# A decoder block on one core: the pairs of the channel mixer reordered, gelu's product moved to a rotating PSUM bank

## The chip, the cores and the metric

The kernel runs on one core of a Trainium2 chip. The metric is the device time of one execution in microseconds: the median of three runs before is 828.67 us (828.44 to 828.79). Engines are named as the profile names them: PE (TensorE, matmuls) with PEld (its weight loads), DVE (VectorE), ACT (ScalarE), POOL (GpSimd), SP (which issues the transfers).

## The reference

One layer of a hybrid decoder trunk on 512 tokens of 1024 channels. Two mixers and their merge come first, then the part that the change touches, the channel mixer, and a per-layer embedding:

```python
hf = rmsnorm(x, norm_ffn[i])
up = causal_dwconv(hf @ w_up[i], ffn_dw_w[i], ffn_dw_b[i])
gate, val = jnp.split(up, 2, axis=-1)
x = x + (jax.nn.gelu(gate) * val) @ w_down[i]
```

`w_up` is 1024 x 5632 (2816 columns of gate and 2816 of value), `w_down` 2816 x 1024, and the convolution has three taps along the tokens.

## The kernel before

Every product is made of three matmuls of fp32r parts: an operand is cut into a high part (ACT, `hi_of`, L118) and a low part, the operand minus its high part (`lo_of`, L121, on DVE, in one place on POOL), and high x high, high x low and low x high are summed in PSUM.

The channel mixer works in 22 pairs (`Pair`). Pair f makes 128 columns of gate and the 128 columns of value that belong to them, for all 512 tokens. With the inputs split in two halves (blocks of four 128-row tiles), the tokens in two halves of 256 (LO and HI) and gate against value, this is a 2 x 2 by 2 x 2 block product, and it is done with seven block products instead of eight (m1 to m7; each is 4 x 3 = 12 matmuls of 128x128 by 128x256). The price is sums of weight blocks: blocks 11 and 21 are the halves of the gate's columns, 12 and 22 those of the value's; POOL forms t1 and t2 ("a") and t3 and t4 ("b"), four subtractions of 128x512 per pair (L306). So a pair has four weight tiles to cut: "11" (128x1024, blocks 11 and 21), "t12" and "t34" (128x1024, the sums), and "22" (128x512, block 22).

The list `pieces` gives the order in which weights are fetched, summed, cut and used. `Stream` walks it: `pump` issues what has room (at most four cut tiles are held, three buffers `tt` hold sums), `work` emits the next stage of a cut (a high part, or the low part that follows it), `take` and `done` bracket the use of a tile by PE.

A slot is one block product with what is emitted beside it: `slot` calls the product, `st.work()`, the copy given as `then`, `st.pump()` and `step()`, which moves each tail one yield on. In a middle pair the slots are m6, m2, m1 of the next pair, m7, m5 of the next pair, m3, m4. Each pair accumulates in a PSUM bank for gate and one for value; two of each alternate. Of the eight banks the other four rotate (`ps()`). The seeds carry m1 of the next pair into its banks: `seed_value` (L1329) goes to value HI, before m6; `seed_gate` (L1332) to gate LO, before m2. After m6 its result is copied to value LO (L1344), after m7 value HI is copied to gate HI (L1353).

The tail of a pair (`after`) runs beside the next pair: m5 is added to value (DVE L1375), ACT makes the first taps of value (`uv`, L1380) and gate (`ug`, L1382), DVE the other two taps of each (L1367), ACT gelu (L1387), DVE the product (L1389, into `uv` in SBUF), and the product is cut into the operand `a` of the down product. `seed_value` has to wait until uv's taps have read the value bank, `seed_gate` until the product has read the gate bank.

The down product comes in three groups, at pair 8, at pair 15 and at the end (`rows_product`): two sweeps of 512 columns, each over all its weights and four token tiles of 128, and after a sweep `done` adds each tile's bank to the residual (DVE L1259). The next sweep, and the m1 after it, take the same four rotating banks.

Of the kernel before, what the change touches and what calls it, by code (L numbers as in the profile page):

```python
# [83 lines left out]
def block_kernel(ctx: ExitStack, tc: tile.TileContext, x, p, rel_bias, norm_mix, w_in, conv_dw_w, conv_dw_b,  # L84
# [103 lines left out]
    def up_sums(*names):  # L188
        for name, f in names:
            pieces.append(((name, f), None, 4 if name == "22" else KC, P, "add" if name in ("a", "b") else "sum"))  # L190
# [9 lines left out]
    for f in range(1, NF):  # L200
        if f + 1 < NF:
            up_raw(f + 1)
            up_sums(("a", f + 1), ("b", f + 1), ("11", f + 1))
        if f in DOWN_IN:
            f0, f1 = DOWN_IN[f]
            rows_pieces("down%d" % f0, w_down, list(range(f0, f1)))
        up_sums(("t34", f))
        if f + 1 < NF:
            up_sums(("t12", f + 1))
        up_sums(("22", f))  # L210
    rows_pieces("down%d" % FFN_GROUPS[-1][0], w_down, list(range(*FFN_GROUPS[-1])))
    ple_piece(1)
    rows_pieces("gate", w_ple_gate, list(range(KC)))
# [3 lines left out]
    class Stream:  # L217
# [8 lines left out]
        def pump(self, force=False, most=9):  # L226

            most += self.cuts
            while self.stages:
                self.work()  # L230
            while self.cuts < min(self.dmas, most) and (force or self.asked[self.cuts] < self.call):
                i = self.cuts
                key, _, a, b, tag = pieces[i]
                if tag in ("first", "second"):
                    self.blocks(key[1], self.raw[i], tag)
                elif tag == "add":
                    if self.stages or not self.adds:
                        break
                    self.adds -= 1
                    self.add(*key)  # L240
                elif tag == "sum":
                    src, at = self.sums[key]
                    if self.hls >= self.limit or self.call < at:
                        break
                    hl = work("whl", (P, 2, a, b), F32R, tag="whl", bufs=CUT)
                    self.hl[i] = hl
                    self.cut(hl, src, a, nc.gpsimd if key[0] == "22" and key[1] not in DOWN_IN else nc.vector)
                    self.hls += 1
                    self.seconds -= key[0] == "22"
                    self.raws -= key[0] == "11"  # L250
                elif tag is not None:
                    if tag == "whl" and self.hls >= self.limit:
                        break
                    hl = work("whl", (P, 2, a, b), F32R, tag=tag, bufs=CUT if tag == "whl" else 1)
                    self.hl[i] = hl
                    self.cut(hl, self.raw[i], a)
                    self.hls += tag == "whl"
                    self.raws -= key != ("ple", 0)
                self.cuts += 1
            while self.dmas < len(pieces):  # L260
                i = self.dmas
                key, srcs, a, b, tag = pieces[i]
                if tag in ("sum", "add"):
                    self.asked[i] = self.call
                    self.dmas += 1
                    continue
                if key == ("ple", 0):

                    ple[0] = work("ple", (P, NT, 512))
                    raw = ple[0][:, 2:4, :]  # L270
                else:
                    n, home, most = self.raws, "wraw", 2
                    if tag is None:
                        n, home = self.wholes, "pT"
                    elif tag == "second":
                        n, home = self.seconds, "second"
                        if key[1] > 2:
                            home, most = "pT" if key[1] % 2 else "second", 3
                    if n == most:
                        break  # L280
                    raw = work("wraw", (P, a, b), tag=home, bufs=2)
                    self.raws += tag not in (None, "second")
                c = 0
                for src in srcs:
                    n = src.shape[-1]
                    nc.sync.dma_start(raw[:, :, c:c + n], src)
                    c += n
                self.raw[i], self.asked[i] = raw, self.call
                self.seconds += tag == "second"
                self.wholes += tag is None  # L290
                self.dmas += 1
            self.call += 1
# [894 lines left out]
    def rows_product(name, ks, a_of, done, late=None, filler=None, between=None, last=None, banks=None, order=range(NT),  # L1187
# [3 lines left out]
        for n in range(2):  # L1191
# [8 lines left out]
            for i in range(0, len(ks), 2):  # L1200
                kk = ks[i:i + 2]
                st.pump()
                hl = st.take(name, n, ks[i])
                hls.append((kk, hl))
                if n == 0 or late is None:
                    for t in range(NT):
                        part(t, kk, hl)
                        st.work()
                    st.done()
            if n == 0 or late is None:  # L1210
                if late and name != "gate" and not cut_on:
                    st.pump()
                for t in range(NT):
                    done(t, n, o[t])
                    if late and name != "gate" and not cut_on and t == 1:
                        st.work()
                continue
            if between:
# [88 lines left out]
    def fw(k, c):  # L1307
        return ffnw[k // 2][:, (k % 2) * 44 + c:(k % 2) * 44 + c + 1]
# [7 lines left out]
    class Pair:  # L1316


        def __init__(self, f):
            self.f, self.gate, self.value = f, gates[f % 2], values[f % 2]  # L1320
            self.b1 = None

        def m1(self):
            self.first = ps()
# [6 lines left out]
        def seed_gate(self):  # L1331
            nc.scalar.activation(self.gate[:, LO], self.first[:, LO], AF.Copy)  # L1332

        def m5(self):
            self.t12 = st.take("t12", self.f)
            o = ps()
            mm_block(o[:, LO], self.t12, 0, hf["s1"], True)
            self.m5_ = work("m5", (P, 256), tag="sc", bufs=2)
            nc.scalar.activation(self.m5_, o[:, LO], AF.Copy)

        def m6(self):
            mm_block(self.value[:, HI], self.t12, 4, hf["s2"], False)
            st.done()
            nc.scalar.activation(self.value[:, LO], self.value[:, HI], AF.Copy)  # L1344

        def m2(self):
# [22 lines left out]
        def after(self):  # L1369

            f, c = self.f, NF + self.f
            uv, ug = [work(name, (P, 512), tag="S", bufs=8) for name in ("uv", "ug")]
            v = self.value
            halves = lambda a: a.rearrange("p (h t) -> p h t", h=2)
            nc.vector.tensor_tensor(halves(v), halves(v), self.m5_.unsqueeze(1).broadcast_to((P, 2, 256)),  # L1375
                                    op=ALU.add)
            yield
            yield
            yield
            nc.scalar.activation(uv, v, AF.Identity, scale=fw(2, c), bias=fw(3, c))  # L1380
            yield
            nc.scalar.activation(ug, self.gate, AF.Identity, scale=fw(2, f), bias=fw(3, f))  # L1382
            self.taps(uv, v, c)
            yield
            self.taps(ug, self.gate, f)
            yield
            nc.scalar.activation(self.gate, ug, AF.Gelu_apprx_tanh)  # L1387
            yield
            nc.vector.tensor_tensor(uv, self.gate, uv, op=ALU.mult)  # L1389
            yield  # L1390
            a = act[f] = work("a", (P, 2, 512), F32R, tag="act", bufs=8)
            hi_of(a[:, 0], uv)
            yield
            yield
            lo_of(a[:, 1], uv, a[:, 0])

    gain_f = load_gain(norm_ffn)
    for t in range(NT):
# [53 lines left out]
    def slot(product, then=None, cut=True):  # L1452

        product()
        st.work()
        if then:
            then()
        if cut:
            st.pump()
        step()  # L1460
# [10 lines left out]
    for f in range(NF):  # L1471
# [11 lines left out]
        else:  # L1483
            cut = f not in DOWN_IN
            slot(this.m6, cut=cut)
            if f > 1:
                slot(this.m2, cut=cut)
            else:
                step()
            if f + 1 < NF:  # L1490
                coming = pairs[f + 1] = Pair(f + 1)
            if f in DOWN_IN:
                coming.b1 = st.take("11", f + 1)
                step()
                st.pump(most=1)
                step()
                st.work()
                drain()
                down(*DOWN_IN[f], None)
            if f + 1 < NF:  # L1500
                slot(coming.m1)
            slot(this.m7)
            if f + 1 < NF:
                slot(coming.m5, coming.seed_value)
        tails.append(this.after())
        slot(this.m3)
        slot(this.m4, coming.seed_gate if 0 < f < NF - 1 else None)
    drain()
    gain_p = load_gain(norm_ple)
# [89 lines left out]
```

## Time and profile before

| | |
|---|---|
| median of three runs | 828.67 us (828.44 to 828.79) |
| the profiled execution | 829.38 us |
| its span, first to last instruction | 827.6 us |
| granted TensorE clock, mean | 0.997 |
| PE busy | 802.1 us, 97% |
| DVE busy | 606.1 us, 73% |
| ACT busy | 442.8 us, 54% |
| POOL busy | 190.4 us, 23% |
| stage of the pairs and the two downs inside it | 400 to 722 us |

A timeline row reads: start, duration, engine, source line, operation, tile written and tiles read, shapes, and in brackets the idle time of the engine just before with what ended it. A duration includes the time in which an instruction that has started is held back. The distance of two starts on one engine is a little shorter than the duration, since the next instruction begins while the last one still writes. Matmul ends are modelled, so PE is read from start to start.

### The profile page before, as it was taken

Reading aid. Unit: us, or ns where it says so; the run is one execution under the profiler, and the core shown is the slowest. Engines: PE = TensorE matmul, PEld = TensorE weight load, DVE = VectorE, ACT = ScalarE, POOL = GpSimd, SP = SyncE. Lnnn points to the kernel's source line nnn. Section 1 sums busy time; section 2 is a strip of 40 time slices with the busy share of each in tenths; the row PEclk is TensorE's granted clock in tenths of the full one; section 3 lists DMA queues with packets and bytes.
Section 4 is the critical chain, followed back from the end, with each engine's and each line's share of the span. In section 5 each row is a group of like instructions: output and inputs, shape, how many; then the busy total and the mean of one; then the engine's idle time right before and its main releaser. Section 6 shows DMA issues by size and latency. Waiting matters only on the chain.

```text
span 827.6 us, 12258 instructions
## 1 busy us (share of the span) xinstructions
PE 802.1 (97%) x4688; PEld 695.1 (84%) x4688; DVE 606.1 (73%) x965; ACT 442.8 (54%) x839; POOL 190.4 (23%) x183
## 2 busy tenths in 40 slices
PE   7999999999999999999989999999999999999996
PEld 5888888888888876887789998799987899888885
DVE  5469987988987897935779986359984389855664
ACT  6331624287778874432666774147762277634443
POOL 2000000000010000005477661046640266201012
PEclk9999999999999999999999999999999999999998
DMA  7246777411110113452043323413324232231322
GB/s 219 78 119 186 184 191 177 94 52 52 51 51 27 51 52 107 146 205 76 27 129 102 103 77 116 140 51 102 103 77 134 70 104 77 77 127 52 129 75 103
DMA packets 108070, 84.69 MB, mean 102 GB/s; under 512 B 4113, under 2 KB 93641, under 8 KB 108011
## 3 DMA queue, kind: packets, MB, share of 16 engines
q1 hardware_dynamic: 108010, 83.90, 34.7%
q8 instruction: 37, 0.61, 0.3%
q14 instruction: 23, 0.18, 0.1%
HBM read 79.36 MB, written 2.43 MB: 99 GB/s over the span
## 4 chain that ended last, share of the span: by engine, by line
PE 68%; DVE 16%; ACT 9%; issue 3%; POOL 2%; DMA 1%; SPq 0%; POOLq 0%; ACTq 0%; DVEq 0%
PE ps L128 9%; PE ps L130 9%; PE ps L129 9%; PE ps L142 8%; PE ps L143 8%; PE ps L141 8%; ACT whl L118 5%; DVE whl L121 5%; DVE a L121 3%; DVE ug L1367 3%; DVE uv L1367 3%; PE ps L868 2%; PE ps L894 2%; PE ps L135 2%; PE ps L137 2%
## 5 line engine op out<-in xcount | busy, mean ns | idle before, releaser
L121 DVE TENSOR_TENSOR whl<-wraw,whl 128x512 fp32r<-128x512 f32 (+1 forms) x140 | 133.7, 968 | 84.0 <-ACT whl L118 80.5
L135 PE MATMUL ps<-hf,whl 128*128 128x256 f32 x616 | 176.3, 286 | 4.7 <-ACT ps L1332 2.4
L118 ACT ACTIVATE whl<-wraw 128x512 fp32r<-128x512 f32 (+1 forms) x160 | 123.6, 794 | 101.5 <-PE ps L143 36.0
L137 PE MATMUL ps<-hf,whl 128*128 128x256 f32 x616 | 174.7, 284 | 2.3 <-DVE whl L121 1.8
L136 PE MATMUL ps<-hf,whl 128*128 128x256 f32 x616 | 174.2, 283 | 0.0
L135 PEld LDWEIGHTS ps<-hf,whl 128*128 128x128 f32 x616 | 118.0, 192 | 8.5 <-ACT ps L1332 4.8
L137 PEld LDWEIGHTS ps<-hf,whl 128*128 128x128 f32 x616 | 118.1, 192 | 3.2 <-DVE whl L121 2.5
L136 PEld LDWEIGHTS ps<-hf,whl 128*128 128x128 f32 x616 | 118.1, 192 | 0.0
L128 PE MATMUL ps<-hT,whl 128*128 128x512 f32 x256 | 101.9, 398 | 0.0
L130 PE MATMUL ps<-hT,whl 128*128 128x512 f32 x256 | 100.2, 391 | 0.3 <-DVE whl L121 0.3
L129 PE MATMUL ps<-hT,whl 128*128 128x512 f32 x256 | 99.9, 390 | 0.0
L734 DVE SCALAR_TENSOR_TENSOR acc<-aT,convw,acc 128x512 f32<-128x512 f32 x120 | 86.2, 747 | 1.0
L306 POOL TENSOR_TENSOR tt<-wraw 128x512 f32<-128x512 f32 x44 | 65.7, 1494 | 77.1 <-DVE whl L121 71.9
L121 DVE TENSOR_TENSOR whl<-tt,whl 128x1024 fp32r<-128x1024 f32 x44 | 58.5, 1334 | 24.4 <-ACT whl L118 23.8
L142 PE MATMUL ps<-whl,a 128*128 128x512 f32 x176 | 69.6, 396 | 1.2 <-DVE whl L121 1.2
L141 PE MATMUL ps<-whl,a 128*128 128x512 f32 x176 | 69.7, 396 | 0.7 <-DVE x L1259 0.7
L143 PE MATMUL ps<-whl,a 128*128 128x512 f32 x176 | 69.4, 395 | 0.0
L306 POOL TENSOR_TENSOR tt<-wraw,tt 128x512 f32<-128x512 f32 x44 | 60.0, 1364 | 9.3 <-DVE whl L121 6.0
L118 ACT ACTIVATE whl<-tt 128x1024 fp32r<-128x1024 f32 x44 | 46.0, 1045 | 22.0 <-PE ps L143 19.0
L130 PEld LDWEIGHTS ps<-hT,whl 128*128 128x128 f32 x256 | 48.0, 188 | 11.2 <-DVE whl L121 0.7
L128 PEld LDWEIGHTS ps<-hT,whl 128*128 128x128 f32 x256 | 48.1, 188 | 9.0 <-issue 0.2
L129 PEld LDWEIGHTS ps<-hT,whl 128*128 128x128 f32 x256 | 48.2, 188 | 8.7
(214 smaller groups left out, 1529.1 us busy)
## 6 DMA issues: line engine op xcount, KB each, us to landing
wraw<-in_w_up SPq DMA_DIRECT2D x44, 512.0 KB
wraw<-in_w_in SPq DMA_DIRECT2D x32, 512.0 KB
wraw<-in_w_down SPq DMA_DIRECT2D x20, 512.0 KB
wraw<-in_w_out SPq DMA_DIRECT2D x8, 512.0 KB
wraw<-in_w_ple_gate SPq DMA_DIRECT2D x8, 512.0 KB
W<-vdram SPq DMA_DIRECT2D x8, 264.0 KB
xin<-in_x SPq DMA_DIRECT2D x4, 512.0 KB
wraw<-in_w_ck SPq DMA_DIRECT2D x4, 512.0 KB
```

The source lines that it names most:

```text
L118: nc.scalar.activation(dst, src, AF.Copy, scale=scale)
L121: engine.tensor_tensor(dst, src, f32(hi), op=ALU.subtract)
L128: nc.tensor.matmul(o, hl[:, 0, j, cs], a_hi, start=start, stop=False)
L129: nc.tensor.matmul(o, hl[:, 0, j, cs], a_lo, start=False, stop=False)
L130: nc.tensor.matmul(o, hl[:, 1, j, cs], a_hi, start=False, stop=stop)
L135: nc.tensor.matmul(o, hl[:, 0, j0 + k, :], a[:, 0, k, :], start=start and k == 0, stop=False, skip_group_check=True)
L136: nc.tensor.matmul(o, hl[:, 0, j0 + k, :], a[:, 1, k, :], start=False, stop=False, skip_group_check=True)
L137: nc.tensor.matmul(o, hl[:, 1, j0 + k, :], a[:, 0, k, :], start=False, stop=k == 3, skip_group_check=True)
L141: nc.tensor.matmul(o, a_hi, w_hi, start=start, stop=False)
L142: nc.tensor.matmul(o, a_hi, w_lo, start=False, stop=False)
L143: nc.tensor.matmul(o, a_lo, w_hi, start=False, stop=stop)
L306: sub = lambda to, x_, y_: nc.gpsimd.tensor_tensor(to, x_, y_, op=ALU.subtract)
```

## The change

- In the tail, gate comes before value: first taps on ACT, then the taps on DVE; gelu follows ug's taps directly, with uv's taps beside it.
- Gelu's product goes to a rotating PSUM bank instead of `uv`, and the high and low part of `a` are cut from there (not in the last pair before a down and in the last two pairs, which write `uv` as before). High and low part of `a` come one and two yields earlier.
- The low part of block 22 is DVE's in every pair; POOL only makes sums.
- In `slot` the copy (`then`) is emitted before `st.work()`; `seed_value` comes after m3 instead of after m5.
- In `rows_product` a sweep without `late` (the two downs inside) adds the residual of a token tile right after that tile's last product.
- At the end, m1 of the last pair takes the slot of m5 in the pair before it, m5 of the last pair runs in its own pair between m7 and m3, and the pieces "11" and "t12" of the last pair are listed later. `take_t12` lets m5 and m6 come in either order.

What DVE runs in a middle pair, from the product that closes one tail to the taps of the next (before). `whl` is a cut weight tile, `tt` a sum, `wraw` a raw weight, `a` the cut product:

```order
L1389 TENSOR_TENSOR uv_4222<-ps_3343,uv_4222 128x512
L1375 TENSOR_TENSOR ps_3346<-ps_3346,m5_4201 128x512
L121 TENSOR_TENSOR whl_4345<-wraw_4091,whl_4345 128x1024
L121 TENSOR_TENSOR whl_4367<-tt_4167,whl_4367 128x1024
L121 TENSOR_TENSOR whl_4385<-tt_4292,whl_4385 128x1024
L121 TENSOR_TENSOR a_4369<-uv_4222,a_4369 128x512
L1367 SCALAR_TENSOR_TENSOR uv_4350<-ps_3346,ffnw0_819,uv_4350 128x511
L1367 SCALAR_TENSOR_TENSOR uv_4350<-ps_3346,ffnw0_819,uv_4350 128x510
L1367 SCALAR_TENSOR_TENSOR ug_4351<-ps_3344,ffnw0_819,ug_4351 128x511
L1367 SCALAR_TENSOR_TENSOR ug_4351<-ps_3344,ffnw0_819,ug_4351 128x510
```

And after:

```order
L1386 SCALAR_TENSOR_TENSOR uv_4226<-ps_3345,ffnw0_819,uv_4226 128x510
L1410 TENSOR_TENSOR ps_4351<-ps_3343,uv_4226 128x512
L1394 TENSOR_TENSOR ps_3346<-ps_3346,m5_4200 128x512
L121 TENSOR_TENSOR whl_4347<-wraw_4091,whl_4347 128x1024
L121 TENSOR_TENSOR a_4353<-ps_4351,a_4353 128x512
L121 TENSOR_TENSOR whl_4372<-tt_4168,whl_4372 128x1024
L121 TENSOR_TENSOR whl_4389<-tt_4294,whl_4389 128x1024
L121 TENSOR_TENSOR whl_4404<-wraw_4019,whl_4404 128x512
L1386 SCALAR_TENSOR_TENSOR ug_4356<-ps_3344,ffnw0_819,ug_4356 128x511
L1386 SCALAR_TENSOR_TENSOR ug_4356<-ps_3344,ffnw0_819,ug_4356 128x510
L1386 SCALAR_TENSOR_TENSOR uv_4355<-ps_3346,ffnw0_819,uv_4355 128x511
L1386 SCALAR_TENSOR_TENSOR uv_4355<-ps_3346,ffnw0_819,uv_4355 128x510
```

ug's taps stand before uv's, the low part of `a` reads `ps` and stands behind the low part of "11", and a 128x512 low part from `wraw` (block 22) has joined the three others, behind the low part of t12.

ACT in the same stretch before, from the copy of m5 to the high part of block 22:

```order
L1339 ACTIVATE m5_4329<-ps_4316 128x256
L1329 ACTIVATE ps_3345<-ps_4278 128x256
L1387 ACTIVATE ps_3343<-ug_4223 128x512
L118 ACTIVATE whl_4345<-wraw_4091 128x1024
L1332 ACTIVATE ps_3343<-ps_4278 128x256
L118 ACTIVATE whl_4367<-tt_4167 128x1024
L118 ACTIVATE a_4369<-uv_4222 128x512
L1344 ACTIVATE ps_3345<-ps_3345 128x256
L118 ACTIVATE whl_4385<-tt_4292 128x1024
L118 ACTIVATE whl_4400<-wraw_4019 128x512
```

And after:

```order
L1357 ACTIVATE m5_4329<-ps_4316 128x256
L1406 ACTIVATE ps_3343<-ug_4227 128x512
L1339 ACTIVATE ps_3345<-ps_4280 128x256
L118 ACTIVATE whl_4347<-wraw_4091 128x1024
L118 ACTIVATE a_4353<-ps_4351 128x512
L1342 ACTIVATE ps_3343<-ps_4280 128x256
L118 ACTIVATE whl_4372<-tt_4168 128x1024
L1363 ACTIVATE ps_3345<-ps_3345 128x256
L118 ACTIVATE whl_4389<-tt_4294 128x1024
L118 ACTIVATE whl_4404<-wraw_4019 128x512
```

Gelu (L1387, now L1406) stands ahead of value's seed (L1329, now L1339), and the high part of `a` ahead of gate's seed (L1332, now L1342) instead of behind the high part of t34. The sums of POOL keep their order and lose the low part that stood between two pairs' sums; the first sum of a pair still waits for the low part of t34, whose buffer it takes over, and the third for the low part of t12.

The diff:

```diff
@@ -200,14 +200,20 @@
     for f in range(1, NF):
         if f + 1 < NF:
             up_raw(f + 1)
-            up_sums(("a", f + 1), ("b", f + 1), ("11", f + 1))
+            up_sums(("a", f + 1), ("b", f + 1))
+        if f + 2 < NF:
+            up_sums(("11", f + 1))
         if f in DOWN_IN:
             f0, f1 = DOWN_IN[f]
             rows_pieces("down%d" % f0, w_down, list(range(f0, f1)))
         up_sums(("t34", f))
-        if f + 1 < NF:
+        if f + 2 < NF:
             up_sums(("t12", f + 1))
+        if f + 2 == NF:
+            up_sums(("11", f + 1))
         up_sums(("22", f))
+        if f + 2 == NF:
+            up_sums(("t12", f + 1))
     rows_pieces("down%d" % FFN_GROUPS[-1][0], w_down, list(range(*FFN_GROUPS[-1])))
     ple_piece(1)
     rows_pieces("gate", w_ple_gate, list(range(KC)))
@@ -244,7 +250,7 @@
                         break
                     hl = work("whl", (P, 2, a, b), F32R, tag="whl", bufs=CUT)
                     self.hl[i] = hl
-                    self.cut(hl, src, a, nc.gpsimd if key[0] == "22" and key[1] not in DOWN_IN else nc.vector)
+                    self.cut(hl, src, a)
                     self.hls += 1
                     self.seconds -= key[0] == "22"
                     self.raws -= key[0] == "11"
@@ -1205,14 +1211,18 @@
                 if n == 0 or late is None:
                     for t in range(NT):
                         part(t, kk, hl)
+                        if late is None and kk[-1] == ks[-1]:
+                            done(t, n, o[t])
                         st.work()
                     st.done()
-            if n == 0 or late is None:
-                if late and name != "gate" and not cut_on:
+            if late is None:
+                continue
+            if n == 0:
+                if name != "gate" and not cut_on:
                     st.pump()
                 for t in range(NT):
                     done(t, n, o[t])
-                    if late and name != "gate" and not cut_on and t == 1:
+                    if name != "gate" and not cut_on and t == 1:
                         st.work()
                 continue
             if between:
@@ -1318,7 +1328,7 @@
 
         def __init__(self, f):
             self.f, self.gate, self.value = f, gates[f % 2], values[f % 2]
-            self.b1 = None
+            self.b1 = self.t12 = None
 
         def m1(self):
             self.first = ps()
@@ -1331,16 +1341,25 @@
         def seed_gate(self):
             nc.scalar.activation(self.gate[:, LO], self.first[:, LO], AF.Copy)
 
+        def take_t12(self):
+
+            if self.t12 is None:
+                self.t12 = st.take("t12", self.f)
+                return lambda: None
+            return st.done
+
         def m5(self):
-            self.t12 = st.take("t12", self.f)
+            used = self.take_t12()
             o = ps()
             mm_block(o[:, LO], self.t12, 0, hf["s1"], True)
+            used()
             self.m5_ = work("m5", (P, 256), tag="sc", bufs=2)
             nc.scalar.activation(self.m5_, o[:, LO], AF.Copy)
 
         def m6(self):
+            used = self.take_t12()
             mm_block(self.value[:, HI], self.t12, 4, hf["s2"], False)
-            st.done()
+            used()
             nc.scalar.activation(self.value[:, LO], self.value[:, HI], AF.Copy)
 
         def m2(self):
@@ -1377,22 +1396,22 @@
             yield
             yield
             yield
+            nc.scalar.activation(ug, self.gate, AF.Identity, scale=fw(2, f), bias=fw(3, f))
+            yield
             nc.scalar.activation(uv, v, AF.Identity, scale=fw(2, c), bias=fw(3, c))
-            yield
-            nc.scalar.activation(ug, self.gate, AF.Identity, scale=fw(2, f), bias=fw(3, f))
-            self.taps(uv, v, c)
             yield
             self.taps(ug, self.gate, f)
             yield
+            self.taps(uv, v, c)
             nc.scalar.activation(self.gate, ug, AF.Gelu_apprx_tanh)
             yield
-            nc.vector.tensor_tensor(uv, self.gate, uv, op=ALU.mult)
+
+            o = uv if f + 1 in DOWN_IN or f >= NF - 2 else ps()
+            nc.vector.tensor_tensor(o, self.gate, uv, op=ALU.mult)
+            a = act[f] = work("a", (P, 2, 512), F32R, tag="act", bufs=8)
+            hi_of(a[:, 0], o)
             yield
-            a = act[f] = work("a", (P, 2, 512), F32R, tag="act", bufs=8)
-            hi_of(a[:, 0], uv)
-            yield
-            yield
-            lo_of(a[:, 1], uv, a[:, 0])
+            lo_of(a[:, 1], o, a[:, 0])
 
     gain_f = load_gain(norm_ffn)
     for t in range(NT):
@@ -1452,9 +1471,9 @@
     def slot(product, then=None, cut=True):
 
         product()
-        st.work()
         if then:
             then()
+        st.work()
         if cut:
             st.pump()
         step()
@@ -1484,7 +1503,7 @@
             cut = f not in DOWN_IN
             slot(this.m6, cut=cut)
             if f > 1:
-                slot(this.m2, cut=cut)
+                slot(this.m2, cut=cut and f + 1 < NF)
             else:
                 step()
             if f + 1 < NF:
@@ -1492,18 +1511,21 @@
             if f in DOWN_IN:
                 coming.b1 = st.take("11", f + 1)
                 step()
+                step()
                 st.pump(most=1)
                 step()
                 st.work()
                 drain()
                 down(*DOWN_IN[f], None)
-            if f + 1 < NF:
+
+            if f + 2 < NF:
                 slot(coming.m1)
+            else:
+                step()
             slot(this.m7)
-            if f + 1 < NF:
-                slot(coming.m5, coming.seed_value)
+            slot(coming.m5 if f + 2 < NF else coming.m1 if f + 1 < NF else this.m5)
         tails.append(this.after())
-        slot(this.m3)
+        slot(this.m3, coming.seed_value if 0 < f < NF - 1 else None)
         slot(this.m4, coming.seed_gate if 0 < f < NF - 1 else None)
     drain()
     gain_p = load_gain(norm_ple)
```

## Rows read from the trace of the kernel before

**Rows 1.** Waits of the weight loads, 400 to 730 us: total us, times, longest.
```profile
PEld ps L135 <- ACT ps L1332: 4.8, 11, 0.9
...
PEld ps L135 <- ACT ps L1353: 2.0, 2, 1.3
...
PEld ps L142 <- DVE whl L121: 1.9, 2, 0.9
```

**Rows 2.** Timeline of PE, two starts of m2: start us, duration us, instruction.
```profile
478.72 0.39 PE L135 MATMUL ps<-hf,whl 128*128 128x256 f32 x1 [0.21 <-ACT ps L1332]
...
488.66 0.28 PE L136 MATMUL ps<-hf,whl 128*128 128x256 f32 x1
...
488.78 0.28 PE L137 MATMUL ps<-hf,whl 128*128 128x256 f32 x1
...
489.26 0.39 PE L135 MATMUL ps<-hf,whl 128*128 128x256 f32 x1 [0.20 <-ACT ps L1332]
```

**Rows 3.** Timeline of ACT, the same pair.
```profile
485.91 0.37 ACT L1329 ACTIVATE ps<-ps 128x256 f32<-128x256 f32 x1 [0.75 <-DVE uv L1367]
...
487.35 0.60 ACT L1387 ACTIVATE ps<-ug 128x512 f32<-128x512 f32 x1 [1.07 <-DVE ug L1367]
...
487.89 1.04 ACT L118 ACTIVATE whl<-wraw 128x1024 fp32r<-128x1024 f32 x1
...
488.84 0.37 ACT L1332 ACTIVATE ps<-ps 128x256 f32<-128x256 f32 x1
...
489.14 1.04 ACT L118 ACTIVATE whl<-tt 128x1024 fp32r<-128x1024 f32 x1
...
490.08 0.62 ACT L118 ACTIVATE a<-uv 128x512 fp32r<-128x512 f32 x1
...
490.91 1.04 ACT L118 ACTIVATE whl<-tt 128x1024 fp32r<-128x1024 f32 x1
```

**Rows 4.** Timeline of DVE, the same pair.
```profile
484.30 1.52 DVE L1367 SCALAR_TENSOR_TENSOR uv<-ps,ffnw,uv 128x511 f32<-128x511 f32 x2
...
485.74 1.52 DVE L1367 SCALAR_TENSOR_TENSOR ug<-ps,ffnw,ug 128x511 f32<-128x511 f32 x2
...
491.98 1.23 DVE L121 TENSOR_TENSOR whl<-tt,whl 128x1024 fp32r<-128x1024 f32 x1 [0.22 <-ACT whl L118]
...
493.12 1.78 DVE L121 TENSOR_TENSOR a<-uv,a 128x512 fp32r<-128x512 f32 x1
```

**Rows 5.** Timeline of POOL, the same pair.
```profile
492.54 1.82 POOL L121 TENSOR_TENSOR whl<-wraw,whl 128x512 fp32r<-128x512 f32 x1 [3.00 <-ACT whl L118]
```

**Rows 6.** Timeline, a sum of POOL that waited for a low part of DVE.
```profile
534.72 1.22 DVE L121 TENSOR_TENSOR whl<-tt,whl 128x1024 fp32r<-128x1024 f32 x1 [5.31 <-ACT whl L118]
...
536.02 1.30 POOL L306 TENSOR_TENSOR tt<-wraw 128x512 f32<-128x512 f32 x1 [35.97 <-DVE whl L121]
```

**Rows 7.** Timeline of DVE and POOL, two starts close together, and one alone.
```profile
811.45 0.69 DVE L1536 TENSOR_TENSOR x<-x,gain 128x512 f32<-128x512 f32 x1 [0.85 <-ACT junk L418]
...
811.49 0.70 POOL L431 TENSOR_TENSOR rstd<-ss 128x1 f32<-128x1 f32 x1 [4.09 <-ACT junk L418]
...
771.07 0.19 POOL L431 TENSOR_TENSOR rstd<-ss 128x1 f32<-128x1 f32 x1 [6.42 <-ACT junk L418]
```

**Rows 8.** Timeline of POOL and ACT, pair 1.
```profile
427.43 2.27 POOL L306 TENSOR_TENSOR tt<-wraw 128x512 f32<-128x512 f32 x1
...
431.52 1.28 ACT L1387 ACT_TABLE_LOAD   x1 [0.46 <-DVE ug L1367]
```

**Rows 9.** Timeline of PE, between the two sweeps of the first down.
```profile
521.48 0.39 PE L143 MATMUL ps<-whl,a 128*128 128x512 f32 x1
...
522.20 0.47 PE L141 MATMUL ps<-whl,a 128*128 128x512 f32 x1 [0.33 <-DVE x L1259]
```

**Rows 10.** Timeline of DVE, the pair after the first down.
```profile
550.87 1.23 DVE L121 TENSOR_TENSOR whl<-tt,whl 128x1024 fp32r<-128x1024 f32 x1 [0.28 <-ACT whl L118]
...
552.52 1.23 DVE L121 TENSOR_TENSOR whl<-tt,whl 128x1024 fp32r<-128x1024 f32 x1 [0.42 <-ACT whl L118]
```

## The prediction

> **What bounds the kernel now.** I read the page's busy line first: TensorE is busy nearly all the time, so time can come only out of its gaps. The waits of its weight loads in the stage of the pairs [rows 1] list those gaps by releaser: 11 of 4.8 us together end with the copy of L1332 (the gate's seed, before m2); two of 1.9 with the low part of a down's first block (L142); the longest of L1353, 1.3, is in the last pair.
>
> A middle pair [rows 2]: matmuls of 256 columns start 0.12 us apart (488.66, 488.78), so a pair's 84 take 10.08. From one m2 to the next (478.72 to 489.26) it takes 10.54. The difference, 0.46, is one stop before m2.
>
> What sets 10.54 is a loop through the other engines [rows 3 to 5]. Gelu waits for ug's second tap (485.74 + 1.52); then ScalarE runs without a break (hi of "11", gate's seed, hi of t34, hi of a, the copy of value, hi of t12, ending 491.95). VectorE starts t12's low part at 491.98. GpSimd's low part of block 22, started at 492.54, ends at 494.36, 1.15 after VectorE's 493.21. The low part of a, started at 493.12, ends at 494.90, 0.54 after GpSimd's. Each was held until the other engine's instruction was over. Then four taps, and the loop is closed.
>
> **The change, part by part.** I rebuild that loop from the same rows, in the order that the section on the change shows.
>
> 1. *The pair's loop.* ug's taps now come first, so gelu runs beside uv's taps and leaves the loop. From the end of uv's second tap: value's seed starts 0.09 later (485.82 to 485.91); to the next start it takes 0.30 (as 488.84 to 489.14), hi of "11" 0.95 (487.89 to 488.84), hi of a and the copy of value 0.83 (490.08 to 490.91), gate's seed 0.30, hi of t34 0.94 (489.14 to 490.08), hi of t12 1.04, and 0.03 to VectorE: 4.48. Then t12's low part, 1.23, to 5.71.
>
> Here the fourth low part (block 22) has become VectorE's, and GpSimd's sums wait for nothing but t34's low part (and for transfers of a loop earlier). Hi of t34 ends at 0.09 + 0.30 + 0.95 + 0.53 + 0.30 + 1.04 = 3.21, its low part at 3.21 + 0.03 + 1.22 = 4.46, and GpSimd starts 0.08 after such an end [rows 6], at 4.54. VectorE starts t12's low part at 4.48, 0.06 earlier, so I take it that VectorE goes first and the sum is held until 5.71 + 1.15 = 6.86. The fourth low part queues behind that sum and ends 0.54 later, at 7.40; the next instruction starts 0.09 earlier (493.21, 493.12), and uv's second tap ends 1.44 (484.30 to 485.74) + 1.52 after that: 10.27. The other three sums run beside taps, as sums do now. So the loop goes from 10.54 to 10.27, and TensorE still stops 0.19 per pair.
>
> Does a lead of 0.06 decide? At 811.45 VectorE started a product of two SBUF tiles, and 0.04 later GpSimd a tiny tensor_tensor: it took 0.70 where it takes 0.19 alone [rows 7], so with that lead VectorE was served first.
>
> The Trainium skill (Perfetto Trace Analysis, GPSIMD Engine Instruction) calls the span of a GpSimd instruction in a profile unreliable, which speaks against reading 0.06 us off such rows. By that sentence the first rival below would be as likely as the forecast; no run here shows the rule itself.
>
> 2. *Gelu's product in PSUM.* No row has the product into PSUM with hi and low part read from it. The nearest are hi of a from SBUF, 0.62, and a tap that reads PSUM, 0.76 (half of 1.52): I take the first, and up to 0.14 more per pair is in the range, since hi of a is on the loop. The low part of a has one SBUF operand left and, like the taps, should not be held; it is off the loop, as t34's low part waits for ScalarE to within 0.03 with it. The bank is one of three that a pair takes in turn from four; its readers are done some 7 us before it is taken again. Cost 0.
>
> 3. *The first pairs.* The fourth low part of pair 1 runs on VectorE as soon as the sum of 427.43 + 2.27 ends [rows 8], by 430.25; the stop of m3 that now waits for GpSimd there goes. But value's seed stands behind gelu, and the first gelu has the table load, 1.28. ug's second tap ends 0.54 - 0.09 + 1.52 after 429.70, at 431.67; + 0.09 + 1.28 + 0.54 puts the seed at 433.6. From there I run the loop once; the first sums last until 435.4 and hold the low part of "11", by which t34's slips 0.25. So the next seed starts at 433.6 + 10.27 + 0.2 = 444.05, the gate's seed 0.30 + 0.95 + 0.53 later, and m2 of pair 3 at 445.83 + 0.37 + 0.05 = 446.2. Before, it is 489.26 - 4 x 10.54 = 447.1. Gain 0.9.
>
> 4. *Pairs 4 to 8:* 5 x (10.27 - 10.54) = -1.3.
>
> 5. *The two downs inside.* The residual add follows each token tile's last product instead of all four, so its bank is free when the next sweep begins, under the matmuls of three other tiles. Four stops go. Each costs between the 0.33 of idle that its row shows and the 0.72 from the matmul before it [rows 9]; I take 0.55, so -2.2 (-1.3 to -2.9). The down's first low part takes the place of t34's and ends 4.46 after the tap; TensorE begins the down at 0.09 + 1.78 + 0.42 + 12 x 0.12 = 3.7, and its second matmul needs that low part. The stop falls from 0.95 [rows 1] to 0.6, twice: -0.7.
>
> 6. *Group 2 (pairs 9 to 15).* After a down TensorE is the late one. Before, that lead lasted four pairs, and then three of the 11 stops cost 1.3. After, the first loop has t34's low part end at 550.87 + 1.23 and a sum start at 552.18, ahead of t12's low part (552.52, since hi of t12 waits for m6) [rows 10]. There GpSimd goes first, the lead is eaten in one pair, and there is one stop of about 0.4, then 5 x 0.19: 1.3. So 0.
>
> 7. *Group 3.* Before: two of the 11, 0.8, and the 1.3 of L1353. After: 0.4 + 3 x 0.19; then pairs 20 and 21 with six blocks each and no sums. m5 of pair 21 now covers L1353; m1 of pair 21 has moved between m7 and m3 of pair 20, so the seeds come late by 0.1, 0.2 and 0.3 by the same row lengths. 1.5 against 2.1: -0.6.
>
> Sum: -0.9 - 1.3 - 2.2 - 0.7 - 0.6 = -5.7. The profiled execution took 829.38 (span 827.60 and 1.78 around it), which gives 823.7; the median of the runs is 0.71 below it, 828.67, so I predict **823.0**.
>
> **Rivals.**
>
> *GpSimd's sum goes first in every pair (slower).* If the 0.06 is lost, t12's low part waits for one more sum, 1.2 us, and the loop is 11.5. That is 0.95 above before: pairs 4 to 8 +4.7; group 2, 0.4 + 5 x 1.4 against 1.3: +6.1; group 3, 0.4 + 3 x 1.4 + 0.6 against 2.1: +3.1; items 3 and 5 stay, -3.8. Sum +10.1: **838.8**. What decides: which of the two starts first behind t34's low part. For it: the lead is that of two row ends, and after each down it happens. Against it: rows 7, and that any delay of t34's low part moves the sum back too.
>
> *GpSimd first in about half of the pairs:* 13 loops, half of them 1.2 longer, 7.8 on top of -5.7: **830.8**.
>
> *The fourth low part is not held.* If the sum came behind it, the loop would be 10.27 - 1.15 = 9.1, below TensorE's 10.08, and the pairs would run without stops: -0.9 - 2.3 - 2.9 - 1.3 - 1.5 = -8.9, **819.8**. Against it: at 492.54 and 493.12 the engine that waited was served before the one that had just finished.
>
> *Nothing comes of it.* If the seeds arrive no earlier and the stops at the residual adds move to the low parts behind them, 828.5. Against it: the row at 522.20 names the add itself.
>
> **How the numbers follow.** Forecast 0.60 (own range 820.5 to 826: 0.14 more in the loop is 1.8 us, item 5 is good to +0.9 and -0.7, the first and last pairs to 0.5 each); GpSimd first throughout 0.18; in half 0.06; not held 0.12; nothing 0.04. What a measurement can tell from no change is about 0.2%, 1.7 us. Faster: 0.60 + 0.12 + a third of the half case = 0.74; same: 0.04 + 0.02 = 0.06; slower: 0.18 + 0.02 = 0.20. The range reaches from below 819.8 to just above the half case, 818 to 831.5, and leaves out 838.8.
>
> **What would show it.** In a middle pair of the profile after: m2 to m2 10.27 (11.5 if the first rival holds, 10.08 if the low part is not held); t12's low part 1.23 and the first sum held to 2.3 (the rival: low part 2.4, sum 1.3); the fourth low part about 1.8; a's low part near 0.7 instead of 1.78; gelu over before uv's second tap; no wait for a residual add; none for the copy of value in the last pair. It would be wrong if m6 rather than m2 stops, or if the product or hi of a take more than 0.76.

## The result and the profile after

The changed kernel takes **823.76 us** (median, 823.02 to 824.31); the kernel before took 828.56 beside it. The ratio is 0.9944, 95% interval 0.9927 to 0.9961: faster by 0.6%. The profiled execution took 823.72 (span 821.9, granted clock 0.997 as before).

First the waits of the weight loads after, in the window of [rows 1]: what was waited for, total us, times, longest.

```profile
PEld ps L142 <- DVE whl L121: 1.2, 2, 0.6
PEld ps L135 <- ACT ps L1342: 1.2, 5, 0.3
PEld ps L135 <- ACT ps L1339: 1.0, 1, 1.0
PEld ps L135 <- ACT ps L1372: 0.7, 1, 0.7
```

L1342 is the gate's seed (L1332 before): 4.8 us of waits in eleven places have become 1.2 in five. The wait of 1.3 for the copy of value in the last pair is gone, that for a down's first low part (L142) fell from 1.9 to 1.2, and one wait of 1.0 for the value's seed (L1339) is new. Short stops do not appear in this list: TensorE still stops in every middle pair, as the next rows show.

Next a middle pair after. TensorE, from one m2 to the next (start us, duration, instruction):

```profile
476.98 0.39 PE L135 MATMUL ps<-hf,whl 128*128 128x256 f32 x1
...
487.04 0.28 PE L137 MATMUL ps<-hf,whl 128*128 128x256 f32 x1
487.23 0.39 PE L135 MATMUL ps<-hf,whl 128*128 128x256 f32 x1
```

The period is 10.25 where [rows 2] have 10.54, and the stop before m2 is still there, but short: 487.04 to 487.23 is 0.19 where a start without a stop comes after 0.12, so 0.07 late. The next matmul is 0.10 late as well; together that is the 0.17 by which the pair exceeds 10.08.

ScalarE, VectorE and GpSimd in the same pair:

```profile
483.64 0.60 ACT L1406 ACTIVATE ps<-ug 128x512 f32<-128x512 f32 x1 [0.22 <-DVE ug L1386]
485.08 0.37 ACT L1339 ACTIVATE ps<-ps 128x256 f32<-128x256 f32 x1 [0.84 <-DVE uv L1386]
...
486.31 0.59 ACT L118 ACTIVATE a<-ps 128x512 fp32r<-128x512 f32 x1
486.79 0.39 ACT L1342 ACTIVATE ps<-ps 128x256 f32<-128x256 f32 x1
```

```profile
487.59 0.68 DVE L121 TENSOR_TENSOR a<-ps,a 128x512 fp32r<-128x512 f32 x1
488.19 2.46 DVE L121 TENSOR_TENSOR whl<-tt,whl 128x1024 fp32r<-128x1024 f32 x2
490.57 1.78 DVE L121 TENSOR_TENSOR whl<-wraw,whl 128x512 fp32r<-128x512 f32 x1
492.27 1.52 DVE L1386 SCALAR_TENSOR_TENSOR ug<-ps,ffnw,ug 128x511 f32<-128x511 f32 x2
```

```profile
489.49 2.31 POOL L312 TENSOR_TENSOR tt<-wraw 128x512 f32<-128x512 f32 x1 [3.59 <-DVE whl L121]
...
494.85 1.30 POOL L312 TENSOR_TENSOR tt<-wraw 128x512 f32<-128x512 f32 x1
```

Gelu (483.64) is over before uv's second tap, which ends just ahead of the value's seed at 485.08. The two low parts of 2.46 are t34's and t12's, 1.23 each, so that t12's starts at 489.42 (488.19 + 2.46 - 1.23). GpSimd's first sum starts 0.07 later, at 489.49, and is held: 2.31, against 1.30 for the last sum, which runs beside taps. The fourth low part is held in turn behind that sum: 1.78, where a's low part of the same size, with one operand in PSUM and no sum beside it, takes 0.68 (1.78 in [rows 4]).

Then the stage of the pairs and the downs by its first matmuls; L135 begins a group of pairs, L141 the down behind it.

```profile
403.33 0.38 PE L135 MATMUL ps<-hf,whl 128*128 128x256 f32 x1
...
499.02 0.40 PE L141 MATMUL ps<-whl,a 128*128 128x512 f32 x1
499.71 0.50 PE L142 MATMUL ps<-whl,a 128*128 128x512 f32 x1 [0.30 <-DVE whl L121]
...
518.88 0.39 PE L143 MATMUL ps<-whl,a 128*128 128x512 f32 x1
519.11 0.39 PE L141 MATMUL ps<-whl,a 128*128 128x512 f32 x1
...
538.63 0.28 PE L135 MATMUL ps<-hf,whl 128*128 128x256 f32 x1
...
610.47 0.40 PE L141 MATMUL ps<-whl,a 128*128 128x512 f32 x1
...
650.08 0.28 PE L135 MATMUL ps<-hf,whl 128*128 128x256 f32 x1
...
716.46 0.39 PE L141 MATMUL ps<-whl,a 128*128 128x512 f32 x1
```

Before, the same starts are:

```profile
403.66 0.39 PE L135 MATMUL ps<-hf,whl 128*128 128x256 f32 x1
...
501.32 0.40 PE L141 MATMUL ps<-whl,a 128*128 128x512 f32 x1
...
542.23 0.39 PE L135 MATMUL ps<-hf,whl 128*128 128x256 f32 x1 [0.27 <-DVE x L1259]
...
614.17 0.40 PE L141 MATMUL ps<-whl,a 128*128 128x512 f32 x1
...
655.08 0.39 PE L135 MATMUL ps<-hf,whl 128*128 128x256 f32 x1 [0.26 <-DVE x L1259]
...
722.12 0.39 PE L141 MATMUL ps<-whl,a 128*128 128x512 f32 x1
```

The differences, against the terms predicted:

| part of the stage | before | after | difference | predicted |
|---|---|---|---|---|
| group 1, to the first down | 97.66 | 95.69 | -1.97 | -2.2 (items 3, 4) |
| first down | 40.91 | 39.61 | -1.30 | -1.45 (item 5) |
| group 2 | 71.94 | 71.84 | -0.10 | 0 (item 6) |
| second down | 40.91 | 39.61 | -1.30 | -1.45 (item 5) |
| group 3 | 67.04 | 66.38 | -0.66 | -0.6 (item 7) |
| sum | 318.46 | 313.13 | -5.33 | -5.7 |

Between the two sweeps of the first down (518.88 to 519.11) TensorE goes on in 0.23; the stop of [rows 9] is gone.

### The profile page after: what moved, and what is told of

The parts are those of the page before. It is cut to its first block, busy times and chain, and to the rows that moved or that the text cites. A ratio compares the mean times of both kernels' runs of the same rounds, so it can differ in the third digit from the quotient of the medians.

```text
span 821.9 us, 12322 instructions
## 1 busy us (share of the span) xinstructions
PE 802.6 (98%) x4688; PEld 696.2 (85%) x4688; DVE 618.8 (75%) x985; ACT 441.9 (54%) x839; POOL 170.5 (21%) x163
## 4 chain that ended last, share of the span: by engine, by line
PE 74%; DVE 12%; ACT 6%; issue 4%; POOL 2%; DMA 1%; SPq 0%; POOLq 0%; ACTq 0%; DVEq 0%
PE ps L128 9%; PE ps L130 9%; PE ps L129 9%; PE ps L142 9%; PE ps L143 8%; PE ps L141 8%; DVE whl L121 5%; PE ps L135 3%; ACT whl L118 3%; PE ps L136 3%; PE ps L137 3%; PE ps L874 2%; PE ps L900 2%; DVE ug L1386 2%; DVE uv L1386 2%
## 5 line engine op out<-in xcount | busy, mean ns | idle before, releaser
L121 DVE TENSOR_TENSOR whl<-wraw,whl 128x512 fp32r<-128x512 f32 (+1 forms) x160 | 165.0, 1040 | 78.1 <-ACT whl L118 75.5
L135 PE MATMUL ps<-hf,whl 128*128 128x256 f32 x616 | 177.4, 288 | 1.5 <-ACT ps L1339 0.8
L135 PEld LDWEIGHTS ps<-hf,whl 128*128 128x128 f32 x616 | 117.9, 191 | 5.5 <-ACT ps L1342 1.2
L312 POOL TENSOR_TENSOR tt<-wraw 128x512 f32<-128x512 f32 x44 | 72.7, 1652 | 148.1 <-DVE whl L121 140.3
L142 PE MATMUL ps<-whl,a 128*128 128x512 f32 x176 | 69.7, 396 | 0.6 <-DVE whl L121 0.6
L141 PE MATMUL ps<-whl,a 128*128 128x512 f32 x176 | 69.6, 396 | 0.0
L312 POOL TENSOR_TENSOR tt<-wraw,tt 128x512 f32<-128x512 f32 x44 | 66.6, 1514 | 9.5 <-DVE whl L121 6.2
L121 DVE TENSOR_TENSOR whl<-tt,whl 128x1024 fp32r<-128x1024 f32 x44 | 56.9, 1297 | 12.6 <-ACT whl L118 12.1
```

Of the source, the lines that this page charges most:

```text
L121: engine.tensor_tensor(dst, src, f32(hi), op=ALU.subtract)
L135: nc.tensor.matmul(o, hl[:, 0, j0 + k, :], a[:, 0, k, :], start=start and k == 0, stop=False, skip_group_check=True)
L141: nc.tensor.matmul(o, a_hi, w_hi, start=start, stop=False)
L142: nc.tensor.matmul(o, a_hi, w_lo, start=False, stop=False)
L312: sub = lambda to, x_, y_: nc.gpsimd.tensor_tensor(to, x_, y_, op=ALU.subtract)
```

## The experiments

Each is an edit of the changed kernel; lines inserted shift the line numbers of some. The second measure beside the time is the stage, as in the table's last row, read from each trace; it leaves out what the chip and the rest of the program add. It is one execution of each kernel, but a part that an edit does not touch repeats closely: the first down takes 39.61 in the changed kernel and in e_product_sbuf, 39.60 in e_last and e_uv_first. The intervals of the four runs at 0.9922 to 0.9929 overlap that of the changed kernel, so what is said of their gains of 1.9 to 2.5 us rests on the stage. The kernel before was timed anew beside each set of experiments (827.07 to 828.36), so the ratios are to be compared, not the medians.

| kernel | us | ratio to before (95%) | stage us | against after |
|---|---|---|---|---|
| changed kernel | 823.76 | 0.9944 (0.9927 to 0.9961) | 313.13 | |
| e_act_delay | 839.67 | 1.0142 (1.0127 to 1.0158) | 329.40 | +16.27 |
| e_delay_wait | 821.26 | 0.9929 (0.9916 to 0.9941) | 310.99 | -2.14 |
| e_sums_wait | 821.82 | 0.9929 (0.9917 to 0.9942) | 311.27 | -1.86 |
| e_low_pool | 821.61 | 0.9926 (0.9914 to 0.9938) | 311.20 | -1.93 |
| e_best | 820.89 | 0.9922 (0.9910 to 0.9934) | 310.65 | -2.48 |
| e_uv_first | 833.67 | 1.0072 (1.0059 to 1.0085) | 324.77 | +11.64 |
| e_resid | 825.02 | 0.9962 (0.9949 to 0.9975) | 315.18 | +2.05 |
| e_product_sbuf | 823.76 | 0.9948 (0.9934 to 0.9963) | 313.58 | +0.45 |
| e_last | 823.56 | 0.9943 (0.9930 to 0.9956) | 313.43 | +0.30 |

**e_act_delay: does the lead of 0.07 us decide?**

```
+ if key[0] == "t12":
+     nc.scalar.activation(hl[:, 1, 0, 0:64], src[:, 0, 0:64], AF.Copy)
  self.cut(hl, src, a)
```

> A copy of 64 columns is put on ScalarE ahead of the high part of t12, so that this high part ends about 0.2 to 0.25 us later and VectorE's low part of t12 starts behind GpSimd's first sum, not 0.07 us ahead of it (468.92 against 468.99 in the pair at 468 us). Theory (the order of these two starts decides who is held): the first sum runs in about 1.3 us and VectorE's low part of t12 in about 2.4, the fourth low part is held again behind the second sum; the pair's loop grows by 1.2 to 2.4 us and TensorE stops for as much in about 15 pairs: 842 us, 836 to 860. Rival (the order does not matter, the delay alone goes through): 0.2 us in 15 pairs, 827 us.

The copy's target is filled by the low part afterwards. It took 839.67, 16 us more. A middle pair of it, VectorE's t12 low part, GpSimd's sums and the small copy on ScalarE (a pair later):

```profile
471.37 2.29 DVE L121 TENSOR_TENSOR whl<-tt,whl 128x1024 fp32r<-128x1024 f32 x1 [0.17 <-ACT whl L118]
```

```profile
471.29 1.29 POOL L314 TENSOR_TENSOR tt<-wraw 128x512 f32<-128x512 f32 x1 [4.97 <-DVE whl L121]
...
482.74 1.30 POOL L314 TENSOR_TENSOR tt<-wraw 128x512 f32<-128x512 f32 x1 [4.98 <-DVE whl L121]
```

```profile
481.60 0.25 ACT L254 ACTIVATE whl<-tt 128x64 fp32r<-128x64 f32 x1
```

Now the sum is first by 0.08 and runs free, and t12's low part is held, 2.29. The pair takes 11.45 (471.29 to 482.74), 1.20 more than 10.25, from a copy whose cost on ScalarE is 0.14 (481.60 to the next start, 481.74). That is the forecast's first rival, which I had put at 838.8, 10.1 above the kernel before; here it is 12.1 above the 827.57 measured beside it. The rival here, the delay alone, falls.

**e_sums_wait and e_delay_wait: GpSimd's sums wait for the fourth low part, without and with the small copy.**

```
  def add(self, name, f):
+     if name == "a" and self.low22 is not None:
+         nc.gpsimd.tensor_copy(to[:, 0, 0:1], self.low22.bitcast(F32))
+         self.low22 = None
  ...
  self.cut(hl, src, a)
+ if key[0] == "22":
+     self.low22 = hl[:, 1, 0, 0:1]
```

> A copy of one column on GpSimd, from the fourth low part (block 22's) into the tile that the first sum writes, stands ahead of the first sum, so that GpSimd's sums wait for the fourth low part. Theory: the fourth low part is no longer held (1.78 us becomes 0.68), the first sum neither (2.31 becomes 1.3), the loop loses 1.1 us and is under TensorE's 10.08; the sums end about 1 us later, just ahead of the high part of t34: 820 to 822 us. Rival: the sums then end too late for t34, and the last of them meets the low part of block 11 on VectorE: TensorE stops at m7 by some 0.3 us per pair, 825 to 829 us.

> Both edits at once: the copy of 64 columns on ScalarE ahead of t12's high part, and GpSimd's sums made to wait for the fourth low part. Theory (the 16 us that the small copy cost by itself come from the first sum's start ahead of t12's low part): with the sums behind the fourth low part nothing is left to win that race, and the small copy costs at most its own 0.14 to 0.25 us in each of some 17 pairs beside the 821.8 us of the waiting sums: 822 to 826 us. Rival (the copy costs what it costs by ScalarE's chain, whoever goes first): 837 to 838 us.

The waiting sums take 1.86 us off the stage. In e_sums_wait, VectorE and GpSimd:

```profile
475.20 2.37 DVE L121 TENSOR_TENSOR whl<-wraw,whl 128x1024 fp32r<-128x1024 f32 x1
...
480.36 0.68 DVE L121 TENSOR_TENSOR whl<-wraw,whl 128x512 fp32r<-128x512 f32 x1
```

```profile
475.20 1.29 POOL L317 TENSOR_TENSOR tt<-wraw 128x512 f32<-128x512 f32 x1
481.11 0.18 POOL L315 COPY tt<-whl 128x1 f32<-128x1 f32 x1 [4.62 <-DVE whl L121]
481.37 1.30 POOL L317 TENSOR_TENSOR tt<-wraw 128x512 f32<-128x512 f32 x1
```

The fourth low part is down to 0.68 and the first sum to 1.30. The later sums meet the next pair's first low part instead (475.20 on both, and VectorE is held), but there the hold costs less: the middle pairs take 10.18 (471.19 to 481.37 between first sums), and behind the downs 10.08 (m2 at 557.37 and 567.45). The forecast's rival without the hold was 3.2 below the forecast (-8.9 against -5.7), and the three groups of pairs do take 3.06 less than in the changed kernel. The two downs take 1.20 of it back: L142's waits rise from 1.2 to 2.4 us. Ahead of the first down the low part of "11" is held by the last sum (2.38 at 495.58), and the down's first low part comes behind it.

With the small copy added the time does not rise (310.99 against 311.27), where by itself the copy cost 16.27. So it was the order of the two starts that cost it, and the rival, ScalarE's chain, falls. It is even 0.28 under. In the pair shown the last sum is now the one that is held, and not VectorE's first low part, but the two starts lie too close together to call it a lead, and that this is where the 0.28 comes from is not shown:

```profile
475.22 1.23 DVE L121 TENSOR_TENSOR whl<-wraw,whl 128x1024 fp32r<-128x1024 f32 x1
```

```profile
475.23 2.38 POOL L319 TENSOR_TENSOR tt<-wraw 128x512 f32<-128x512 f32 x1
```

**e_low_pool and e_best: block 22's low part back on GpSimd.**

```
- self.cut(hl, src, a)
+ self.cut(hl, src, a, nc.gpsimd if key[0] == "22" and key[1] not in DOWN_IN else nc.vector)
```

e_best adds `and key[1] < NF - 2` to the condition.

> The low part of block 22 goes back to GpSimd, ahead of its sums; all else stays. Theory (the pair's loop, which holds the fourth low part of 1.78 us on VectorE, stops TensorE 0.18 us per pair at the value's seed): the taps follow t12's low part directly, the loop falls from 10.25 us to under TensorE's own 10.08, the stop of 0.18 us goes in about 15 pairs, and the sums, which start 1.1 us later, still end just ahead of the high part of t34: 820 to 821.5 us. Rival (the gain of the change came from taking this low part off GpSimd): slower than the changed kernel, 826 to 830 us, with stops at m7 or at block 22's product.

> Block 22's low part on GpSimd in all pairs but the two behind the downs and the last two. In the trace with it on GpSimd throughout, TensorE stops 0.57 and 0.19 us in the last two pairs, for the value's and the gate's seed, against 0.10 and 0.19 in the changed kernel. Theory (the low part on GpSimd belongs to these stops): 0.5 us off 821.6: 821.1 us. Rival (the stop there has another cause): 821.6 us.

Both beat the changed kernel's stage, by 1.93 and 2.48. (The stop of 0.18 that the first expectation puts at the value's seed is the one before m2, at the gate's seed.) This part of the change, taken by itself, costs time: on GpSimd the low part stands ahead of the sums and makes them wait, as the one-column copy did, and VectorE's loop loses one instruction. In the pair shown GpSimd's low part goes first and t12's, the second of VectorE's two, is held (2.31 at 477.84). Most middle pairs take TensorE's own 10.08 (m2 at 455.23, 465.31 and 475.39); the pair shown, like one middle pair of each other group, takes 0.35 more, and TensorE stops in it (m2 at 475.39 and 485.82):

```profile
476.71 3.45 DVE L121 TENSOR_TENSOR whl<-tt,whl 128x1024 fp32r<-128x1024 f32 x2
```

```profile
477.74 1.33 POOL L121 TENSOR_TENSOR whl<-wraw,whl 128x512 fp32r<-128x512 f32 x1 [2.64 <-ACT whl L118]
479.03 2.27 POOL L312 TENSOR_TENSOR tt<-wraw 128x512 f32<-128x512 f32 x1
```

Of e_best's 0.55 the trace shows the cause, the stop at m6 of the last pair is gone; the two runs' intervals overlap, so its time alone does not show it. The stop in e_low_pool, and the same place in e_best:

```profile
704.74 0.38 PE L135 MATMUL ps<-hf,whl 128*128 128x256 f32 x1 [0.41 <-ACT ps L1339]
```

```profile
705.06 0.39 PE L135 MATMUL ps<-hf,whl 128*128 128x256 f32 x1
```

e_best, with the lowest ratio and the shortest stage of all, is the version to keep, though the times alone do not set it apart from e_low_pool and the two runs with waiting sums.

**e_uv_first: the value's taps first again.**

```
- nc.scalar.activation(ug, ...); yield; nc.scalar.activation(uv, ...); yield
- self.taps(ug, self.gate, f); yield; self.taps(uv, v, c)
+ nc.scalar.activation(uv, ...); yield; nc.scalar.activation(ug, ...); yield
+ self.taps(uv, v, c); yield; self.taps(ug, self.gate, f)
  nc.scalar.activation(self.gate, ug, AF.Gelu_apprx_tanh)
```

> The value's taps and their activation stand ahead of the gate's again, and gelu behind the gate's taps, which end last; all else as in the changed kernel. Theory: the chain from the end of the last taps now holds gelu, the product and the high part of a ahead of the gate's seed, while the value's seed and block 11's high part may go ahead: 0.1 to 0.5 us per pair longer than the loop of 10.25, 825 to 828 us. Rival (the order of the taps does nothing): 823.8 us.

It took 833.67, more than I had expected: I had let the value's seed go ahead of gelu, and it doesn't. ScalarE and VectorE:

```profile
477.98 0.60 ACT L1406 ACTIVATE ps<-ug 128x512 f32<-128x512 f32 x1 [1.66 <-DVE ug L1386]
478.52 0.34 ACT L1339 ACTIVATE ps<-ps 128x256 f32<-128x256 f32 x1
```

```profile
478.62 0.70 DVE L1410 TENSOR_TENSOR ps<-ps,uv 128x512 f32<-128x512 f32 x1 [0.73 <-ACT ps L1406]
```

Gelu starts behind ug's second tap; the value's seed queues behind it on ScalarE, and VectorE idles 0.73 for the product. The pair takes 10.77 by the first sums (472.13 to 482.90), 0.52 more than 10.25. TensorE waits 17 times for that seed; 0.52 in 16 of them is 8.3 of the 11.64, and the longer wait at the first (2.4 against 1.0) is another 1.4; the rest I have not traced. The run undoes only half of the new order: in the kernel before, the value's seed stood ahead of gelu, and here it stays behind it, so that the time is above that of the kernel before. What it shows is that, with gelu ahead of the value's seed, the gate's taps have to come first; what the order of the taps is worth with the seeds as before was not run.

**e_resid, e_product_sbuf, e_last: the smaller parts.**

```
e_resid
-         if late is None and kk[-1] == ks[-1]:
-             done(t, n, o[t])
  if late is None:
+     for t in range(NT):
+         done(t, n, o[t])
      continue
e_product_sbuf
- o = uv if f + 1 in DOWN_IN or f >= NF - 2 else ps()
+ o = uv
e_last (also: "11" and "t12" of the last pair listed as before)
- if f + 2 < NF: slot(coming.m1)
+ if f + 1 < NF: slot(coming.m1)
  slot(this.m7)
- slot(coming.m5 if f + 2 < NF else coming.m1 if f + 1 < NF else this.m5)
+ if f + 1 < NF: slot(coming.m5)
```

> The residual adds of a down product stand behind all four row tiles again, not each behind its own. Theory (term of the sum: four stops of 0.55 us at the first products behind a down): 2.2 us slower than the changed kernel, 826.0 us. Rival (the stops were hidden by the loop and are made up again in the next pair): 823.8 us.

> Gelu's product is written over uv in SBUF in all pairs, not into a PSUM bank. Theory (a's low part stands where no sum runs, so that it reads two tiles of SBUF without being held, 0.7 to 0.9 us): 823.8 us, 823 to 825.5. Rival (the bank is what took 1.1 us off a's low part, 1.78 before and 0.68 after): 1.1 us per pair more on the loop, 835 to 842 us.

> The last two pairs in the order of before (m1 of pair 21 ahead of m7 of pair 20, its m5 behind it, block 11 and t12 cut in the old order); all else as in the changed kernel. Theory (term of the sum: 0.6 us): 824.4 us. Rival (the reordering of the last pairs does nothing, or the stop of before had another cause): 823.8 us.

e_resid: the four stops are back, 2.05 on the stage, 0.51 each; the ratios give about 1.5 (0.9962 against 0.9944). One of them:

```profile
519.53 0.47 PE L141 MATMUL ps<-whl,a 128*128 128x512 f32 x1 [0.31 <-DVE x L1269]
```

e_product_sbuf: no difference in the time. a's low part reads two tiles of SBUF and takes 0.69, as from PSUM, since no sum runs beside it; ScalarE's high part of a is 0.62 here and 0.59 from PSUM, and 0.03 in about 15 pairs is the 0.45 of the stage. So a's place in the pair, not the bank, took the hold off it:

```profile
486.39 0.69 DVE L121 TENSOR_TENSOR a<-uv,a 128x512 fp32r<-128x512 f32 x1
```

e_last: the old order costs 0.3 on the stage and nothing that the medians show. The stop at the copy of value is back, but at 0.66 of idle, not the 1.06 of before: the rest of the change had already shortened it.

```profile
713.08 0.39 PE L135 MATMUL ps<-hf,whl 128*128 128x256 f32 x1 [0.66 <-ACT ps L1368]
```

## Why the prediction was right

*Item 1, the pair's loop.* 10.27 predicted, 10.25 measured; the lead of t12's low part 0.06 against 0.07; first sum held (2.31), fourth low part 1.78, TensorE's stop at m2 as forecast. That the order of these two starts decides is shown from both sides by e_act_delay and e_delay_wait. The Trainium skill (Perfetto Trace Analysis, GPSIMD Engine Instruction) calls the span of a GpSimd instruction unreliable; here its recorded start named the engine that was held at leads of 0.07, 0.08 and 0.10 us. At 0.01 it can be wrong: in e_low_pool VectorE is recorded at 433.15 and GpSimd at 433.16, and it is VectorE that is held (2.37). How long a held span is, is another matter: it contains the wait.

*Item 2, gelu's product.* Cost 0 as forecast; its bank gave 0.03 per pair.

*Items 3 and 4, group 1.* The value's seed ends behind gelu and its table load, as worked out, and m2 of pair 3 starts at 446.23 where I had 446.2. That agreement is in part luck: the stage itself began 0.33 earlier than before (403.33 against 403.66), and among the kept traces its start varies from 402.12 to 403.66. From the start of the stage, m2 of pair 3 comes after 42.90, and after 43.43 before (447.09 less 403.66). So item 3 gained 0.53, not 0.9; pairs 4 to 8 gained 1.45 (five times 10.54 less 10.25) where I had 1.3.

```profile
431.83 1.28 ACT L1406 ACT_TABLE_LOAD   x1 [1.28 <-DVE ug L1386]
433.13 0.60 ACT L1406 ACTIVATE ps<-ug 128x512 f32<-128x512 f32 x1
433.66 0.34 ACT L1339 ACTIVATE ps<-ps 128x256 f32<-128x256 f32 x1
```

```profile
446.23 0.39 PE L135 MATMUL ps<-hf,whl 128*128 128x256 f32 x1
```

*Item 5, the downs.* -1.30 each against -1.45; the residual stops were worth 0.5, not 0.55, and the first low part 0.33, not 0.35.

*Item 6, group 2.* As forecast: behind the first down GpSimd's first sum starts at 548.47, ahead of t12's low part at 548.82, which is held (2.04); the first pair takes 10.44 (m2 at 547.25 and 557.69) and the pairs after it 10.25.

*Item 7, the last group.* The sum was right (-0.66 against -0.6), the reason only in part: e_last leaves at most half of it to the new order of the last two pairs.

The stage fell by 5.33 where the sum was 5.7; that the profiled execution fell by 5.66 owes 0.33 to the earlier start of the stage. The medians moved by 4.8, so that the predicted 823.0 stands 0.8 below the median, at the lowest of its runs (823.02). What I had not asked is whether every part of the change gains. The low part taken off GpSimd loses about 2 us of the stage, which the other parts pay for. The value's seed behind m3 and the copies ahead of `st.work()` stand in every run, so that their share is not shown.

## What to carry to other kernels

Where VectorE and GpSimd both read two tiles of SBUF, ask which starts first, from the ends of what releases them: a lead of less than 0.1 us decided here which of them waited out the instruction of the other, 1.2 us in every pair. If the wrong one wins on the loop that sets the period, make the other engine's work wait for the end of the first one's, and check that it still has time for it. And undo the parts of a redesign one by one, also when the whole is faster.

## What the runs showed of the hardware

A held instruction waited for one instruction of the other engine, not for its queue: in the rows the two take turns. In the changed kernel t12's low part (1.23) is not held, the first sum waits for it (2.31), the fourth low part waits for the sum (1.78), and only then GpSimd's next sum goes. The Trainium skill (SBUF — State Buffer, Who interferes with whom) says that a VectorE instruction with two inputs in SBUF contends with a GpSimd instruction that reads SBUF; the rows agree, 1.78 against 0.68 for the same operation beside a sum and without one (e_sums_wait's fourth low part). A small instruction on a third engine, 0.14 us on ScalarE, cost 16 us by changing whose turn is first, and nothing once the turn was fixed by a wait.
